# State-space layer: rows normed in three groups, norm weights multiplied on GpSimd and the scale applied on VectorE

## The chip, the cores and the metric

The kernel runs on one core of one Trainium2 chip. The metric is the device time of one execution in microseconds (us). The kernel before has a median of 1499.05 us over three executions (1498.17 to 1500.22). A core has a matmul engine (TensorE, PE in the rows, with its weight loads as PEld), a vector engine (VectorE, DVE), a scalar engine (ScalarE, ACT), a general engine (GpSimd, POOL) and a queue of DMA issues on SyncE (SP). Each engine works through its own queue of instructions in order; an instruction whose input is late holds everything behind it on that engine.

## The reference, cut to what matters

One inference step of a small decoder: one S5 state-space layer, then shared keys and values, then one layer of stick-breaking attention, over 1024 prompt rows and 8 x 8 sample rows of width 1024. Only the start of the state-space layer is touched:

```python
def _rms_norm(x, g):
    y = x32 * lax.rsqrt(jnp.mean(x32 * x32, axis=-1, keepdims=True) + RMS_EPS)
    return (y * g.astype(jnp.float32)).astype(x.dtype)

def _s5_layer(x, ...):
    h = _rms_norm(x, g_pre)
    uz = h @ w_in                      # 1024 x 2048
    u, z = uz[..., :SSM_WIDTH], uz[..., SSM_WIDTH:]
    y, hr, hi = _s5_scan(u, ...)       # needs lam = exp(dt * a), so exp, sin and cos of 64 x 64 parameters
```

## The kernel before, in words

**Tiles of the norm.** The prompt is read as eight tiles t = 0 to 7 of 128 rows x 1024 (`xt`), and the 64 sample rows are a ninth tile, t = 8, which goes first (line 229). For each tile the loop does: one load on SP's queue (line 232); a Square with row sums on ScalarE (line 240); the inverse root of the mean square, `rstd`, called with GpSimd as its engine, so six small operations of one column on GpSimd (lines 77 to 83: a memset, scale and add, a power, and one Newton step of four operations); then one VectorE instruction that multiplies the row scale `rt` and the norm weights `gpre` into the tile (line 243). Eight TensorE transposes of 128 x 128 follow (line 249), in two banks of PSUM (`psb`, three buffers, and `psa`, two). From each bank ScalarE copies a rounded part `xh` (lines 256 and 261) and VectorE subtracts it to get the remainder `xl` (line 205, the helper `tt`). The tile `xt` has five buffers, so that the loads of t = 4 to 7 wait for a tile to be used up.

**What follows.** `xh` and `xl` come in three chunks of columns: chunk 0 has t = 0 to 2, chunk 1 has t = 3 to 5, chunk 2 has t = 6 and 7, each with its part of the samples. A projection `gemm_u(ft)` takes one 128-column block of the weights, split into `whi_u` (ScalarE, line 140) and `wlo_u` (VectorE, line 141), two buffers each, and runs 24 matmuls on each chunk (lines 147 to 149). The third block's `whi_u` needs a buffer that the first block's last matmul frees.

**The parameters.** Beside the norm VectorE computes exp, angles and powers of the layer's parameters (`s5_params`, lines 91 to 1271). ScalarE's Sin (line 1231, after a table load) stands between them. Out of the results come `uu`, and out of `uu` the table `cs` of each round (line 205 in the loop over `ft`), which is copied to `cf` by DMA. `cs` has one buffer, so that the next round's `cs` waits for that copy.

**What sets the order.** The code is traced in the order in which it is written, and a scheduler then places the instructions of each engine by dependencies, its own estimates and the priorities that the code gives (`high_priority`). Queues are in order at run time.

Of the kernel before, what the change touches and what calls it, by code (L numbers as in the profile page):

```python
# [10 lines left out]
F32 = mybir.dt.float32  # L11
# [3 lines left out]
AF = mybir.ActivationFunctionType  # L15
ALU = mybir.AluOpType
# [3 lines left out]
D = 1024  # L20
SEQ = 1024
NS = 8
TS = 8
NTS = NS * TS
L = 8
NC = SEQ // L
W = NC + NS
# [14 lines left out]
ACH = ((0, 3), (3, 3), (6, 2))  # L42
# [27 lines left out]
def rstd(nc, pool, ss, out, n, mul, tag, eng=None):  # L70

    E = eng or nc.vector
    v = pool.tile([128, n], F32, name=f"v_{tag}", tag="rs_v")
    r0 = pool.tile([128, n], F32, name=f"r0_{tag}", tag="rs_r")
    h = pool.tile([128, n], F32, name=f"h_{tag}", tag="rs_h")
    e = pool.tile([128, n], F32, name=f"e_{tag}", tag="rs_e")
    nc.gpsimd.memset(e, -0.5)
    E.tensor_scalar(v, ss, mul, EPS, op0=ALU.mult, op1=ALU.add)
    nc.gpsimd.tensor_tensor(r0, v, e, op=ALU.pow)
    E.tensor_tensor(h, r0, r0, op=ALU.mult)  # L80
    E.tensor_tensor(h, h, v, op=ALU.mult)
    E.tensor_scalar(h, h, -0.5, 1.5, op0=ALU.mult, op1=ALU.add)
    E.tensor_tensor(out, r0, h, op=ALU.mult)
# [117 lines left out]
def s5_layer(tc, nc, io, wp, bank, cst, gains, ident, sgn, zs_d, u_d, y_d, s2):  # L201
    V, Q = nc.vector, nc.gpsimd

    def tt(eng, o, a, b, op):
        eng.tensor_tensor(o, a, b, op=op)

    with ExitStack() as sx:
# [3 lines left out]
        par = st.enter_context(tc.tile_pool(name="a_par", bufs=1, reuse_waits="tile"))  # L211
        s0 = st.enter_context(ExitStack())
        start = s0.enter_context(tc.tile_pool(name="a_start", bufs=1, reuse_waits="tile"))

        def weights(which, ft):

            with tc.high_priority(2 * OFA):
                wraw = wp.tile([128, KT, 128], F32, name=f"wraw_{which}{ft}", tag="wraw", bufs=1)

                (nc.scalar if which == "u" else nc.sync).dma_start(wraw, io["a_win"][ft + (KT if which == "z" else 0)])  # L220
                return split_w(nc, wp, wraw, f"{which}{ft}", [128, KT, 128], Q if which == "z" and ft % 2 else V)


        gpre = start.tile([128, D], F32, name="gpre")
        xh = [big.tile([128, KT, n, W], F32R, name=f"xh{i}") for i, (_, n) in enumerate(ACH)]
        xl = [big.tile([128, KT, n, W], F32R, name=f"xl{i}") for i, (_, n) in enumerate(ACH)]
        xp = io["x_prompt"].rearrange("(c t) d -> t c d", t=L)
        w_first = None
        for t in (8, 0, 1, 2, 3, 4, 5, 6, 7):
            n = 128 if t < 8 else NTS  # L230
            xt = start.tile([128, D], F32, name=f"xt{t}", tag="xt", bufs=5)
            nc.sync.dma_start(xt[:n], xp[t] if t < 8 else io["x_sample"])
            if t == 8:
                nc.sync.dma_start(gpre, io["a_gpre"].to_broadcast([128, D]))
                nc.sync.dma_start(cst, io["consts"][:, 0:129])
            sq = start.tile([128, D], F32, name=f"sq{t}", tag="sq")
            ss = par.tile([128, 1], F32, name=f"ss{t}", tag="ss", bufs=2)
            if n < 128:
                V.memset(ss, 1024.0)
            nc.scalar.activation(sq[:n], xt[:n], AF.Square, accum_out=ss[:n])  # L240
            rt = par.tile([128, 1], F32, name=f"rt{t}", tag="rt", bufs=2)
            rstd(nc, par, ss, rt, 1, 1.0 / D, f"a{t}", Q)
            V.scalar_tensor_tensor(xt[:n], xt[:n], rt[:n], gpre[:n], op0=ALU.mult, op1=ALU.mult)
            for i in range(2):
                ps = bank("a" if i else "b")
                p3 = ps.rearrange("p (a b) -> p a b", a=4)[:, :, :n]
                for j in range(4):
                    k = 4 * i + j
                    nc.tensor.transpose(p3[:, j], xt[:n, k * 128 : (k + 1) * 128], ident[:n, :n])
                ks = slice(4 * i, 4 * i + 4)  # L250
                for c, (t0, m) in enumerate(ACH):
                    if t < 8:
                        if not t0 <= t < t0 + m:
                            continue
                        src, oh, ol = p3, xh[c][:, ks, t - t0, 0:NC], xl[c][:, ks, t - t0, 0:NC]
                        nc.scalar.activation(oh, src, AF.Copy)
                        tt(V, ol, src, oh, ALU.subtract)
                    else:
                        p4 = p3.rearrange("p a (s t) -> p a t s", t=TS)
                        src, oh, ol = p4[:, :, t0 : t0 + m], xh[c][:, ks, :, NC:W], xl[c][:, ks, :, NC:W]  # L260
                        nc.scalar.activation(oh, src, AF.Copy)
                        tt(V, ol, src, oh, ALU.subtract)
            if t == 0:
                w_first = weights("u", 0)

        def gemm(which, ft, evac, w=None):
            wh, wl = w or weights(which, ft)
# [49 lines left out]
        for ft in range(KT):  # L317
            with tc.high_priority(OFA):
# [19 lines left out]
                for i in range(2):  # L338
                    ps = bank("m")
# [11 lines left out]
                ps = bank("m")  # L351
# [1048 lines left out]
```

## Time and profile before

| what | number |
|---|---|
| median of three executions | 1499.05 us |
| the profiled execution's own time | 1500.17 us |
| its span | 1498.4 us |
| busy on PE, DVE, ACT, POOL | 1415.8, 935.0, 718.2, 493.7 us |
| share of the chain that ended last, PE / DVE / POOL / DMA | 75% / 9% / 5% / 4% |

The span is what the trace covers, and 1.8 us of the execution lie outside it. A row of a timeline gives the start, the duration, the engine, the line, the operation, what is written <- what is read, the shape and the count; in brackets stands how long the engine had been idle and what ended that.

### The profile page before, as it was taken

To read this page: it belongs to the slowest core of one execution; us is meant where nothing else is said; L and a number is where in the kernel's file an instruction comes from. 1 tells how busy PE (TensorE), PEld (TensorE's weight loads), DVE (VectorE), ACT (ScalarE), POOL (GpSimd) and SP (SyncE) were. 2 spreads that over 40 slices of the span, in tenths; PEclk is the share of its full clock that TensorE was granted. 3 is DMA by queue.
4 is the path that set the end of the run, shared out by engine and by line. 5 is a ranking of instruction groups with operands and counts; after the bars stand their busy time and mean duration, and the time that the engine had idled before them with its cause. 6 is when DMAs were issued, how large, how long until landed. Compare 5 with 4: busy or idle time off the path is not lost.

```text
span 1498.4 us, 26819 instructions
## 1 busy us (share of the span) xinstructions
PE 1415.8 (94%) x9648; PEld 1145.8 (76%) x9648; DVE 935.0 (62%) x1506; ACT 718.2 (48%) x1424; POOL 493.7 (33%) x473
## 2 busy tenths in 40 slices
PE   4987988899999989999999999999998999998997
PEld 3987978899977889999988877666565665565766
DVE  6877887758755531110122149897888888789545
ACT  5233454454434433332333347676665766576321
POOL 6556565325412132222111012433323233334200
PEclk9999999999999999999999999999999999999999
DMA  5345556674134252232288755979878686754026
GB/s 197 103 129 139 140 126 163 145 251 145 58 106 132 91 224 91 85 123 100 103 314 298 255 201 192 339 284 326 295 257 289 250 308 219 268 190 139 11 82 213
DMA packets 129670, 276.41 MB, mean 184 GB/s; under 512 B 21633, under 2 KB 66562, under 8 KB 129538
## 3 DMA queue, kind: packets, MB, share of 16 engines
q1 hardware_dynamic: 127234, 268.41, 54.0%
q10 hardware_dynamic: 2304, 6.29, 1.3%
q8 instruction: 76, 1.25, 0.3%
q14 instruction: 56, 0.46, 0.1%
HBM read 224.55 MB, written 39.35 MB: 176 GB/s over the span
## 4 chain that ended last, share of the span: by engine, by line
PE 75%; DVE 9%; POOL 5%; DMA 4%; issue 3%; ACT 2%; SPq 1%; DVEq 0%; POOLq 0%; ACTq 0%
PE psmm L147 7%; PE psmm L149 7%; PE psmm L148 7%; PE psqk L147 6%; PE psqk L148 6%; PE psqk L149 6%; PE psa L949 5%; PE psb L1182 5%; PE psb L1164 4%; PE psa L990 4%; PE psqk L1139 3%; PE psqk L1140 2%; DMA cf<-cs 2%; PE psa L147 2%; PE psa L149 2%
## 5 line engine op out<-in xcount | busy, mean ns | idle before, releaser
L1120 POOL TENSOR_TENSOR ql<-q,qh 128x256 fp32r<-128x256 f32 x64 | 62.5, 977 | 285.6 <-ACT qh L1119 246.5
L1141 ACT ACTIVATE F<-psqk,bp 128x384 f32<-128x384 f32 (+2 forms) x192 | 111.3, 580 | 64.6 <-PE psqk L1140 49.2
L1146 DVE TENSOR_TENSOR_SCAN F<-F,maskb 128x256 f32<-128x256 f32 (+3 forms) x128 | 131.2, 1030 | 14.0 <-ACT F L1141 13.6
L1149 POOL TENSOR_TENSOR S<-S,F 128x255 f32<-128x255 f32 (+3 forms) x64 | 100.8, 1574 | 115.7 <-DVE F L1148 22.5
L1142 ACT ACTIVATE S<-psqk,bp 128x384 f32<-128x384 f32 (+2 forms) x192 | 111.4, 583 | 22.7 <-PE psb L1164 22.6
L1164 PE MATMUL psb<-cst,S 128*128 128x128 f32 x576 | 96.7, 285 | 4.4 <-DVE og L1186 3.8
L1164 PEld LDWEIGHTS psb<-cst,S 128*128 128x128 f32 x576 | 67.3, 143 | 35.1 <-issue 20.5
L1148 DVE TENSOR_TENSOR_SCAN F<-F 128x384 f32<-128x384 f32 (+1 forms) x64 | 78.9, 1233 | 20.4 <-ACT F L1141 19.8
L1182 PE MATMUL psb<-at,vr 128*64 128x256 f32 (+1 forms) x640 | 90.0, 369 | 1.2 <-DVE at L1168 1.2
L949 PE MATMUL psa<-vp,sat 128*32 128x256 f32 x1024 | 86.1, 388 | 0.1
L1139 PE MATMUL psqk<-ks,qh 128*128 128x384 f32 (+2 forms) x192 | 77.4, 404 | 6.9 <-DVE ks L1104 5.2
L990 PE MATMUL psa<-kp,qbd 128*32 128x256 f32 x1024 | 75.5, 389 | 0.5 <-PE psb L1164 0.5
L1182 PEld LDWEIGHTS psb<-at,vr 128*64 128x64 f32 x640 | 46.7, 137 | 36.6 <-issue 10.3
L1168 DVE TENSOR_TENSOR at<-psb,maskb 128x384 f32<-128x384 f32 (+3 forms) x128 | 60.3, 478 | 21.3 <-PE psb L1164 20.7
L147 PE MATMUL psmm<-xh,whi_u 128*128 128x408 f32 (+1 forms) x192 | 65.3, 341 | 3.7 <-ACT ut L278 3.1
L147 PE MATMUL psmm<-x,whi_g 128*128 128x408 f32 (+1 forms) x192 | 66.6, 347 | 1.1 <-DVE gt L739 1.1
L943 DVE TENSOR_TENSOR_SCAN sF<-sF 128x513 f32<-128x513 f32 x32 | 44.4, 1388 | 36.1 <-ACT sF L940 35.8
L1139 PEld LDWEIGHTS psqk<-ks,qh 128*128 128x128 f32 x192 | 37.0, 193 | 37.8 <-ACT S L1142 12.8
L1140 PE MATMUL psqk<-ks,ql 128*128 128x384 f32 (+2 forms) x192 | 65.8, 344 | 0.0
L148 PE MATMUL psmm<-xl,whi_u 128*128 128x408 f32 (+1 forms) x192 | 65.4, 341 | 0.0
L149 PE MATMUL psmm<-x,wlo_g 128*128 128x408 f32 (+1 forms) x192 | 64.9, 338 | 0.2 <-DVE wlo_g L141 0.2
L148 PE MATMUL psmm<-x,whi_g 128*128 128x408 f32 (+1 forms) x192 | 65.1, 339 | 0.0
(452 smaller groups left out, 4234.6 us busy)
## 6 DMA issues: line engine op xcount, KB each, us to landing
kp<-cache_kT SPq DMA_DIRECT2D x128, 512.0 KB, 6.0
vp<-cache_v SPq DMA_DIRECT2D x128, 512.0 KB, 5.7
cf<-cs SPq DMA_DIRECT2D x32, 256.0 KB, 5.4
q<-q_d SPq DMA_DIRECT2D x128, 64.0 KB, 4.6
u_d<-ut SPq DMA_DIRECT2D x8, 544.0 KB, 2.8
ug<-u_d SPq DMA_DIRECT2D x64, 68.0 KB, 2.9
y_d<-gt SPq DMA_DIRECT2D x64, 68.0 KB, 2.4
zs_d<-zt SPq DMA_DIRECT2D x8, 544.0 KB, 4.5
```

Of the source, the lines that this page charges most:

```text
L147: nc.tensor.matmul(ps, sh, mh, start=(k == 0), stop=False)
L148: nc.tensor.matmul(ps, sh, ml, start=False, stop=False)
L149: nc.tensor.matmul(ps, sl, mh, start=False, stop=(k == n - 1))
L949: self.nc.tensor.matmul(po[32 * r : 32 * r + 32, 0:256], a[:, 32 * r : 32 * r + 32], rhs[:, r * 256 : (r + 1) * 256], start=start, stop=stop)
L990: nc.tensor.matmul(ps[32 * r : 32 * r + 32, half * 256 : half * 256 + 256], self.qbd[:, 2 * r + e, s, :], kt[:, :, 2 * r + e, :], start=(e ...
L1139: nc.tensor.matmul(ps[:, :m], qh[:, w], ks[:, c0 : c0 + m], start=True, stop=False)
L1141: nc.scalar.activation(F[:, c0 : c0 + m], ps[:, :m], AF.Sigmoid, bias=bp[:, 1, h : h + 1], scale=-0.125)
L1142: nc.scalar.activation(S[:, c0 : c0 + m], ps[:, :m], AF.Sigmoid, bias=bp[:, 0, h : h + 1], scale=0.125)
L1146: V.tensor_tensor_scan(fr, fr, self.maskb[:, 512 - m : 512][:, ::-1], 1.0, ALU.mult, ALU.max)
L1149: (Q if i % 2 else V).tensor_tensor(S[:, 0 : n - 1], S[:, 0 : n - 1], F[:, 1:n], op=ALU.mult)
L1164: nc.tensor.transpose(ps[:, j * 128 : (j + 1) * 128], S[:, (j0 + j) * 128 : (j0 + j + 1) * 128], self.ident)
L1182: nc.tensor.matmul(po[hs, o:256], self.vr[pi][:, j, hs], ats[hh][j // 4][:, j % 4, o:256], start=(j == 0), stop=(j == nj - 1))
```

## The change

Three parts of the norm move. The nine tiles are taken in three groups, (8, 0, 1, 2), (3, 4, 5) and (6, 7). In each group all loads, Squares and a new GpSimd product `xt * gpre` (in place) come first; then one `rstd` for all columns of the group, now on VectorE except for its memset and its power, which stay on GpSimd; then for each tile a VectorE `tensor_scalar` by `rt`, and the transposes as before. `xt` has nine buffers in place of five. `weights("u", 0)` is called behind the first group's `rstd`.

```diff
@@ -70,10 +70,10 @@
 def rstd(nc, pool, ss, out, n, mul, tag, eng=None):
 
     E = eng or nc.vector
-    v = pool.tile([128, n], F32, name=f"v_{tag}", tag="rs_v")
-    r0 = pool.tile([128, n], F32, name=f"r0_{tag}", tag="rs_r")
-    h = pool.tile([128, n], F32, name=f"h_{tag}", tag="rs_h")
-    e = pool.tile([128, n], F32, name=f"e_{tag}", tag="rs_e")
+    v = pool.tile([128, n], F32, name=f"v_{tag}", tag=f"rs_v{n}")
+    r0 = pool.tile([128, n], F32, name=f"r0_{tag}", tag=f"rs_r{n}")
+    h = pool.tile([128, n], F32, name=f"h_{tag}", tag=f"rs_h{n}")
+    e = pool.tile([128, n], F32, name=f"e_{tag}", tag=f"rs_e{n}")
     nc.gpsimd.memset(e, -0.5)
     E.tensor_scalar(v, ss, mul, EPS, op0=ALU.mult, op1=ALU.add)
     nc.gpsimd.tensor_tensor(r0, v, e, op=ALU.pow)
@@ -226,42 +226,49 @@
         xl = [big.tile([128, KT, n, W], F32R, name=f"xl{i}") for i, (_, n) in enumerate(ACH)]
         xp = io["x_prompt"].rearrange("(c t) d -> t c d", t=L)
         w_first = None
-        for t in (8, 0, 1, 2, 3, 4, 5, 6, 7):
-            n = 128 if t < 8 else NTS
-            xt = start.tile([128, D], F32, name=f"xt{t}", tag="xt", bufs=5)
-            nc.sync.dma_start(xt[:n], xp[t] if t < 8 else io["x_sample"])
-            if t == 8:
-                nc.sync.dma_start(gpre, io["a_gpre"].to_broadcast([128, D]))
-                nc.sync.dma_start(cst, io["consts"][:, 0:129])
-            sq = start.tile([128, D], F32, name=f"sq{t}", tag="sq")
-            ss = par.tile([128, 1], F32, name=f"ss{t}", tag="ss", bufs=2)
-            if n < 128:
-                V.memset(ss, 1024.0)
-            nc.scalar.activation(sq[:n], xt[:n], AF.Square, accum_out=ss[:n])
-            rt = par.tile([128, 1], F32, name=f"rt{t}", tag="rt", bufs=2)
-            rstd(nc, par, ss, rt, 1, 1.0 / D, f"a{t}", Q)
-            V.scalar_tensor_tensor(xt[:n], xt[:n], rt[:n], gpre[:n], op0=ALU.mult, op1=ALU.mult)
-            for i in range(2):
-                ps = bank("a" if i else "b")
-                p3 = ps.rearrange("p (a b) -> p a b", a=4)[:, :, :n]
-                for j in range(4):
-                    k = 4 * i + j
-                    nc.tensor.transpose(p3[:, j], xt[:n, k * 128 : (k + 1) * 128], ident[:n, :n])
-                ks = slice(4 * i, 4 * i + 4)
-                for c, (t0, m) in enumerate(ACH):
-                    if t < 8:
-                        if not t0 <= t < t0 + m:
-                            continue
-                        src, oh, ol = p3, xh[c][:, ks, t - t0, 0:NC], xl[c][:, ks, t - t0, 0:NC]
-                        nc.scalar.activation(oh, src, AF.Copy)
-                        tt(V, ol, src, oh, ALU.subtract)
-                    else:
-                        p4 = p3.rearrange("p a (s t) -> p a t s", t=TS)
-                        src, oh, ol = p4[:, :, t0 : t0 + m], xh[c][:, ks, :, NC:W], xl[c][:, ks, :, NC:W]
-                        nc.scalar.activation(oh, src, AF.Copy)
-                        tt(V, ol, src, oh, ALU.subtract)
-            if t == 0:
+        for group in ((8, 0, 1, 2), (3, 4, 5), (6, 7)):
+
+            xts = {}
+            ss = start.tile([128, len(group)], F32, name=f"ss{group[0]}")
+            rt = start.tile([128, len(group)], F32, name=f"rt{group[0]}")
+            V.memset(ss, 1024.0)
+            for e, t in enumerate(group):
+                n = 128 if t < 8 else NTS
+                xt = start.tile([128, D], F32, name=f"xt{t}", tag="xt", bufs=9)
+                xts[t] = xt
+                nc.sync.dma_start(xt[:n], xp[t] if t < 8 else io["x_sample"])
+                if t == 8:
+                    nc.sync.dma_start(gpre, io["a_gpre"].to_broadcast([128, D]))
+                    nc.sync.dma_start(cst, io["consts"][:, 0:129])
+                sq = start.tile([128, D], F32, name=f"sq{t}", tag="sq")
+                nc.scalar.activation(sq[:n], xt[:n], AF.Square, accum_out=ss[:n, e : e + 1])
+                tt(Q, xt[:n], xt[:n], gpre[:n], ALU.mult)
+            rstd(nc, start, ss, rt, len(group), 1.0 / D, f"a{group[0]}")
+            if group[0] == 8:
                 w_first = weights("u", 0)
+            for e, t in enumerate(group):
+                n = 128 if t < 8 else NTS
+                xt = xts[t]
+                V.tensor_scalar(xt[:n], xt[:n], rt[:n, e : e + 1], None, op0=ALU.mult)
+                for i in range(2):
+                    ps = bank("a" if i else "b")
+                    p3 = ps.rearrange("p (a b) -> p a b", a=4)[:, :, :n]
+                    for j in range(4):
+                        k = 4 * i + j
+                        nc.tensor.transpose(p3[:, j], xt[:n, k * 128 : (k + 1) * 128], ident[:n, :n])
+                    ks = slice(4 * i, 4 * i + 4)
+                    for c, (t0, m) in enumerate(ACH):
+                        if t < 8:
+                            if not t0 <= t < t0 + m:
+                                continue
+                            src, oh, ol = p3, xh[c][:, ks, t - t0, 0:NC], xl[c][:, ks, t - t0, 0:NC]
+                            nc.scalar.activation(oh, src, AF.Copy)
+                            tt(V, ol, src, oh, ALU.subtract)
+                        else:
+                            p4 = p3.rearrange("p a (s t) -> p a t s", t=TS)
+                            src, oh, ol = p4[:, :, t0 : t0 + m], xh[c][:, ks, :, NC:W], xl[c][:, ks, :, NC:W]
+                            nc.scalar.activation(oh, src, AF.Copy)
+                            tt(V, ol, src, oh, ALU.subtract)
 
         def gemm(which, ft, evac, w=None):
             wh, wl = w or weights(which, ft)
```

On GpSimd before, `v_a`, `r_a`, `h_a` and `rt` are the steps of `rstd`, one set for each tile (the first two tiles, t = 8 and t = 0, are shown):

```order
L78 TENSOR_SCALAR v_a_104<-ss_100 128x1
L79 TENSOR_TENSOR r_a_105<-v_a_104,e_a_107 128x1
L80 TENSOR_TENSOR h_a_106<-r_a_105 128x1
L77 MEMSET e_a_147 128x1
L81 TENSOR_TENSOR h_a_106<-h_a_106,v_a_104 128x1
L82 TENSOR_SCALAR h_a_106<-h_a_106 128x1
L83 TENSOR_TENSOR rt_103<-r_a_105,h_a_106 128x1
L78 TENSOR_SCALAR v_a_144<-ss_141 128x1
L79 TENSOR_TENSOR r_a_145<-v_a_144,e_a_147 128x1
```

On GpSimd now, with `xt_98` the sample tile, `xt_105` to `xt_115` t = 0 to 2, `xt_208` to `xt_218` t = 3 to 5, and `xt_282`, `xt_287` t = 6 and 7:

```order
L205 TENSOR_TENSOR xt_105<-xt_105,gpre 128x1024
L205 TENSOR_TENSOR xt_110<-xt_110,gpre 128x1024
L205 TENSOR_TENSOR xt_115<-xt_115,gpre 128x1024
L79 TENSOR_TENSOR r_a_121<-v_a_120,e_a_123 128x4
L205 TENSOR_TENSOR xt_208<-xt_208,gpre 128x1024
L205 TENSOR_TENSOR xt_213<-xt_213,gpre 128x1024
L205 TENSOR_TENSOR xt_218<-xt_218,gpre 128x1024
L79 TENSOR_TENSOR r_a_224<-v_a_223,e_a_226 128x3
L205 TENSOR_TENSOR xt_282<-xt_282,gpre 128x1024
L205 TENSOR_TENSOR xt_287<-xt_287,gpre 128x1024
L1297 COPY pk<-h_509 128x64x8
L79 TENSOR_TENSOR r_a_293<-v_a_292,e_a_295 128x2
```

The products of the second and third group stand directly behind the first group's power, which VectorE waits for. On VectorE before, at the start of the norm (`xt_95` is the sample tile, `xt_138` t = 0):

```order
L141 TENSOR_TENSOR wlo_u_173<-wraw_u_170,whi_u_172 128x1024
L243 SCALAR_TENSOR_TENSOR xt_95<-xt_95,rt_103,gpre 64x1024
L205 TENSOR_TENSOR xl_92<-psb_116,xh_89 128x12x8
L205 TENSOR_TENSOR xl_92<-psa_127,xh_89 128x12x8
L205 TENSOR_TENSOR xl_93<-psb_116,xh_90 128x12x8
L243 SCALAR_TENSOR_TENSOR xt_138<-xt_138,rt_143,gpre 128x1024
```

On VectorE now, at the same place:

```order
L141 TENSOR_TENSOR wlo_u_134<-wraw_u_131,whi_u_133 128x1024
L78 TENSOR_SCALAR v_a_120<-ss_95 128x4
L78 TENSOR_SCALAR v_a_223<-ss_205 128x3
L80 TENSOR_TENSOR h_a_122<-r_a_121 128x4
L81 TENSOR_TENSOR h_a_122<-h_a_122,v_a_120 128x4
L82 TENSOR_SCALAR h_a_122<-h_a_122 128x4
L83 TENSOR_TENSOR rt_96<-r_a_121,h_a_122 128x4
L252 TENSOR_SCALAR xt_98<-xt_98,rt_96 64x1024
L252 TENSOR_SCALAR xt_105<-xt_105,rt_96 128x1024
L252 TENSOR_SCALAR xt_110<-xt_110,rt_96 128x1024
L252 TENSOR_SCALAR xt_115<-xt_115,rt_96 128x1024
L1219 TENSOR_SCALAR aim<-pr,cst 128x64
```

Four tiles are now scaled one behind the other, after four dependent small operations; the first `xl` comes behind them and behind four more instructions.

## Rows read from the trace of the kernel before

**Rows 1.** Chain that ended last, 0 to 75 us: start, duration, what

```profile
23.03 1.54 POOL r_a L79
...
36.83 1.28 DVE xt L243
...
49.71 0.14 PE psmm L148
...
49.87 1.07 ACT whi_u L140
...
50.97 1.23 DVE wlo_u L141
...
52.59 1.28 ACT L1231
...
57.92 3.31 POOL cma_g L126
```

**Rows 2.** Windows: length, busy PE, PEld, DVE, ACT, POOL (count), clock, DMA, GB/s

```profile
80.00:320.00 240.00, 209.97 (x1428) 200.58 (x1427) 180.22 (x302) 107.36 (x239) 130.71 (x101) 0.96 0.58 141
320.00:1498.00 1178.00, 1148.85 (x7901) 891.16 (x7899) 694.45 (x1047) 578.42 (x1124) 317.36 (x273) 0.99 0.56 196
```

**Rows 3.** Timeline of ScalarE, the Square of t = 0

```profile
11.10 1.06 ACT L240 ACTIVATE sq<-xt 128x1024 f32<-128x1024 f32 x1 [2.77 <-DMA xt<-x_prompt]
```

**Rows 4.** The tile of norm weights: its load and landing

```profile
L234 SPq DMA_DIRECT2D gpre<-a_gpre x1: 564/564/564, 1.4 to 1.4; - x1
...
DMA to landing us min/median/max: 6.1/6.1/6.1
```

**Rows 5.** Timeline of GpSimd: a power, a copy, a product of 128 x 1024

```profile
12.61 0.56 POOL L79 TENSOR_TENSOR r_a<-v_a,e_a 128x1 f32<-128x1 f32 x1
...
19.45 0.65 POOL L1290 COPY pk<-h 128x512 f32<-128x512 f32 x1
...
220.46 2.35 POOL L141 TENSOR_TENSOR wlo_z<-wraw_z,whi_z 128x1024 fp32r<-128x1024 f32 x1 [0.55 <-ACT whi_z L140]
```

**Rows 6.** Timeline of VectorE, scales by a column, and t = 2's norm

```profile
16.10 0.24 DVE L1212 TENSOR_SCALAR aim<-pr,cst 128x64 f32<-128x64 f32 x1
...
19.55 1.62 DVE L243 SCALAR_TENSOR_TENSOR xt<-xt,rt,gpre 128x1024 f32<-128x1024 f32 x1
...
120.36 0.33 DVE L328 TENSOR_SCALAR sb<-sb,cst 128x256 f32<-128x256 f32 x1
```

**Rows 7.** Groups by line, VectorE, 0 to 400 us: busy us, mean ns

```profile
L205 DVE TENSOR_TENSOR l<-psb,ts 128x3 f32<-128x3 f32 x16 | 2.4, 150 | 0.0
```

**Rows 8.** Timeline of VectorE and GpSimd side by side, 203 to 212 us

```profile
205.04 1.06 POOL L205 TENSOR_TENSOR m<-uu 128x512 f32<-128x512 f32 x1
205.61 2.17 DVE L205 TENSOR_TENSOR wb<-sb,wri 128x256 f32<-128x256 f32 x2
206.17 1.32 POOL L205 TENSOR_TENSOR cs<-cs,m 128x512 f32<-128x512 f32 x1
...
209.23 1.68 DVE L205 TENSOR_TENSOR ep<-pk,wb 128x1024 f32<-128x1024 f32 x1
209.80 1.71 POOL L205 TENSOR_TENSOR tb<-tb,cf 128x256 f32<-128x256 f32 x1
```

**Rows 9.** Timeline of both engines, three instructions with the other engine out of the way

```profile
66.59 0.30 POOL L131 TENSOR_TENSOR cmc_g<-uu,sc 128x64 f32<-128x64 f32 x1
...
104.87 1.22 DVE L205 TENSOR_TENSOR tm<-pk,wb 128x1024 f32<-128x1024 f32 x1
...
129.70 0.41 DVE L205 TENSOR_TENSOR wb<-sb,wri 128x256 f32<-128x256 f32 x1
```

**Rows 10.** Timeline of VectorE, remainders of t = 6 and 7

```profile
41.81 0.68 DVE L205 TENSOR_TENSOR xl<-psb,xh 128x512 fp32r<-128x512 f32 x1
42.41 0.68 DVE L205 TENSOR_TENSOR xl<-psa,xh 128x512 fp32r<-128x512 f32 x1
```

**Rows 11.** Who waited for whom, 60 to 320 us: total us, times, longest

```profile
PE psa L435 <- ACT gt L437: 10.0, 4, 5.0
```

## The prediction, on record before the changed kernel ran

> **What bounds the kernel now.** I read the windows first. From 320 us on TensorE is busy for 1148.85 of 1178 us, so nothing that happens in the norm can be won or lost there; from 80 to 320 us it is busy for 209.97 of 240, so the state-space rounds have some 30 us in which they wait for something else [rows 2]. Then the chain that ended last, in its first 75 us. The reader is to see three stretches in it. Up to 36.8 us it runs through GpSimd's small operations of the norm, and these are not always cheap: a power takes 1.54 us [rows 1] where another takes 0.56 [rows 5]. Then, from t = 7's norm on VectorE at 36.83, it goes through the remainders and the first block's matmuls, which end at 49.85. At 49.87 ScalarE makes the third block's `whi_u` in the buffer that these matmuls free, VectorE makes `wlo_u` (1.23 us), and ScalarE's table load for Sin begins at 52.59. Behind Sin stand `uu`, `cs` and all rounds [rows 1]. So the change reaches the end only through two moments: when the first block of u is done on TensorE (49.85) and when the table load begins (52.59). I work out where both land.
>
> **What the change removes and adds.** GpSimd loses six small operations for each tile and gets nine products of 128 x 1024. VectorE loses nine instructions that multiply scale and weights at once (1.28 us for the last of them [rows 1], 1.62 for t = 2 [rows 6]) and gets nine scales by a column, three sets of five small operations, and memsets that lie in its idle start. No such product on GpSimd is in the trace of before, but the nearest has the same shape: 2.35 us [rows 5]. A VectorE scale of 128 x 1024 isn't there either. From below: 0.24 us at 64 columns and 0.33 at 256 [rows 6] give 0.47 ns a column, so 0.33 + 768 x 0.47 ns = 0.69 us. From above: 1.28 us, the instruction that it replaces. I take 0.69, since both of its rows are the same operation. A small operation on four columns costs what one on three does, 0.15 us [rows 7]; a power 0.56, and the copy of `h` that now stands in the queue 0.65 [rows 5].
>
> **First group, up to its power.** The norm weights land at 1.4 + 6.1 = 7.5 us [rows 4], and the sample tile's product, 2.35 us, is done by 9.9. The product overwrites its tile, so that t = 0's waits until the Square has read it: 11.10 + 1.06 = 12.2 [rows 3]. Then GpSimd is the bound: t = 0 ends at 14.5, t = 1 at 16.9, `v_a` slips in (0.15), t = 2 ends at 19.4, the power at 20.0. In the kernel before t = 2 was scaled by 19.55 + 1.62 = 21.2 [rows 6]. Up to here there is no loss. The nine loads now stand ahead of the parameters' loads on SP's queue, and none waits for a buffer any more; I cost that at nothing, since VectorE comes to the first of the parameters (`aim`) only behind the four scales. Without that cover it would be up to some 2 us.
>
> **What stands behind that power.** GpSimd goes straight on with the products of t = 3 to 5, the second power, the products of t = 6 and 7 and the copy. VectorE has four small operations that depend on each other, then four scales. Do the two engines run side by side? The trace shows that they don't when both take SBUF tensors: two `wb` that take 0.41 us each alone [rows 9] took 2.17 together. The first waited for GpSimd's `m` to end at 206.10, ran to about 206.4, and the second waited for `cs`, which had got in between and ended at 207.49. `ep` at 209.23 took 1.68 us in place of the 1.22 of a like product (`tm`) alone, and then `tb` on GpSimd was held until `ep` had ended [rows 8, 9]. That is strict turns, one instruction each, though VectorE had the next one ready. So the sum by turns: from 20.0, five products 11.75, a power 0.56, the copy 0.65, four small operations 0.6, four scales 2.76: the first group is scaled at 36.3 us, 15.1 later than before. In this stretch eight instructions of VectorE stand against eight of GpSimd with the first power, so that each finds one ahead of it. Who waits for VectorE there: the transposes of the first group on TensorE, behind them `xh` on ScalarE, and all of the parameters, which are on VectorE itself.
>
> The Trainium skill says the same of the ports: its page "SBUF — State Buffer", section "Who interferes with whom", has it that the pair of ports which VectorE and GpSimd share is a lock held for a whole instruction, taken by a VectorE instruction with two SBUF inputs or in a two-port mode, and that whoever comes second blocks fully. By that rule the sum is the 36.3 above. One row speaks against it as a rule of turns: `cma_g`, 128 x 64, took 3.31 us [rows 1] where its like takes 0.30 alone [rows 9], so GpSimd was kept out through a whole run of short VectorE instructions; by that row VectorE would wait once and then go through.
>
> **From there to the two moments.** Up to the last remainder VectorE has these in its queue: 16 remainders at a pitch of 0.60 [rows 10], 9.6 us; five scales, 3.45; three long ones of about 1.2 (`wlo_u` of the second block, `dd`, its reduction), 3.6; and 57 short ones (the samples' remainders, the exp and angle steps, the two other groups' `rstd`) at 0.15 [rows 7] or a little over, 9.2. That is 26 us without a gap, so the last remainder stands at 62.3. Twelve matmuls of the last chunk are left, at 0.14 each by the row at 49.71 [rows 1], 1.7 us: the first block ends at 64.0 in place of 49.85, 14.1 later. ScalarE's queue now has Sin's table load directly behind the third `whi_u`, so it begins at 64.0 + 1.07 = 65.1 in place of 52.59, 12.5 later; `wlo_u` has gone behind the exp steps and is late for no one but the projection.
>
> Both ends of the unknown: if VectorE waits for GpSimd once and then goes through, the group is scaled at 20.0 + 2.35 + 0.6 + 2.76 = 25.7, and four products, 9.4 us, are left to run beside the rest. The remainders read one tensor from PSUM, and I take them as not held; the other instructions are, so about half of the 9.4 I count as waits: 30.4 in effect, and a table load 6.6 later than before. If nothing waits for anything, the group is scaled at 23.4 and the table load is 0.4 earlier than before. I take 11 us, near the end of strict turns, since rows 8 show turns where GpSimd has a queue of long instructions, which is the case here, and the other row has short ones on both sides.
>
> **Behind the table load.** Everything up to 320 us hangs on Sin's results or on TensorE, and both are late by about the same; I let the delay through whole. Against the profiled execution's own time that is 1500.17 + 11 = 1511.2; the median of the runs lies 1.1 below that execution, so I forecast 1510.
>
> **Rivals.** 1. *Side by side.* GpSimd's products cost VectorE nothing. For it: VectorE's remainders read one tensor from PSUM, and in these it may not meet GpSimd at all. Against: the pairs that met for a turn each [rows 8]. Price: a table load 0.4 earlier, and 2 more if VectorE's 26 us are 24: 1496.7 to 1498.7, no measurable change. 2. *The rounds take it up.* TensorE has 30 idle us between 80 and 320, and if these are waits that a later start does not lengthen, the end moves by 0 to 3: about 1500. Against: the rounds' own chain starts at Sin, and it is late too. 3. *Faster: the new order of the rounds.* The scheduler has reordered them as well; TensorE's state matmuls (`psa`) stood for 10.0 us behind ScalarE's `gt` [rows 11], and if these come at a better place in its queue, all of that goes. With the cheaper end of the norm, 6.6, it is 1499.05 + 6.6 - 10.0 = 1495.7. It decides once more is won there than is lost in front; nothing in the trace of before says that it happens, and the reorder can as well go the other way (1516).
>
> **How the numbers follow.** Turns between the engines 0.70 (1505 to 1514 on its own), a worse order on top of that 0.05 (1516), side by side 0.10, taken up 0.07, faster by the order 0.08. A measurement of this kernel can tell about 0.2% (3 us) from no change, so slower is 0.75, same 0.17, faster 0.08. The range goes from 1498, which leaves out the case of 1495.7 and some of the side by side, to 1516.
>
> **What would show it.** Right: VectorE's four operations behind the first power (lines 80 to 83) start more than 1.5 us apart, each with a product of GpSimd ending before it; the first transposes of t = 2 at about 36 us; the third `whi_u` at about 63 and the table load at about 65; from 320 us on no difference in TensorE's time. Wrong: these four within 1 us, and the table load near 52. Wrong in the second half: a table load 11 us late with an end that is not.

## The result and the profile after

The changed kernel takes 1514.58 us (median of four, 1513.25 to 1515.35), the kernel before 1499.12 us on the same chip (four, 1498.17 to 1500.22): a ratio of 1.0102, 95% interval 1.0084 to 1.0119, so 1.0% slower. 1510 us was forecast, with a range of 1498 to 1516. The profiled execution took 1513.25 us with a span of 1511.5, 13.1 us more than the span before; the medians stand 15.5 apart.

GpSimd's queue in the changed kernel, as a timeline (start, duration, engine, line, operation, what is written <- read, shape, count; in brackets idle time before it):

```profile
12.74 6.96 POOL L205 TENSOR_TENSOR xt<-xt,gpre 128x1024 f32<-128x1024 f32 x3 [2.72 <-ACT sq L244]
19.66 1.03 POOL L79 TENSOR_TENSOR r_a<-v_a,e_a 128x4 f32<-128x4 f32 x1
20.64 6.95 POOL L205 TENSOR_TENSOR xt<-xt,gpre 128x1024 f32<-128x1024 f32 x3
27.53 1.11 POOL L79 TENSOR_TENSOR r_a<-v_a,e_a 128x3 f32<-128x3 f32 x1
28.36 5.22 POOL L205 TENSOR_TENSOR xt<-xt,gpre 128x1024 f32<-128x1024 f32 x2
33.53 1.08 POOL L1297 COPY pk<-h 128x512 f32<-128x512 f32 x1
```

And VectorE's beside it:

```profile
20.72 2.29 DVE L80 TENSOR_TENSOR h_a<-r_a 128x4 f32<-128x4 f32 x1 [0.99 <-POOL r_a L79]
23.05 2.27 DVE L81 TENSOR_TENSOR h_a<-h_a,v_a 128x4 f32<-128x4 f32 x1
25.34 2.27 DVE L82 TENSOR_SCALAR h_a<-h_a 128x4 f32<-128x4 f32 x1
27.65 0.16 DVE L83 TENSOR_TENSOR rt<-r_a,h_a 128x4 f32<-128x4 f32 x1
27.85 7.31 DVE L252 TENSOR_SCALAR xt<-xt,rt 64x1024 f32<-64x1024 f32 x4
```

A product takes 6.96 / 3 = 2.32 us. Each of three operations on four columns, worth 0.16 us, takes 2.3: its product's length. The four scales take 7.31 us, between them two products and the copy. Rows 8 showed turns between instructions of 0.4 to 1.3 us [rows 8]; here the same turns are held by long ones. The three products beside the small operations took 6.95 us, no longer than the three ahead of the power (6.96), so the small operations cost GpSimd nothing. The first group is scaled at 35.16 us; in the kernel before t = 2 was scaled at 21.2 [rows 6].

What TensorE then does, its first transposes:

```profile
28.65 0.69 PE L258 MATMUL psb<-cst,xt 64*128 64x64 f32 x4 [28.65 <-DVE xt L252]
...
31.42 1.11 PE L258 MATMUL psb<-cst,xt 128*128 128x128 f32 x4 [1.66 <-DVE xt L252]
...
34.18 1.12 PE L258 MATMUL psb<-cst,xt 128*128 128x128 f32 x4 [0.80 <-DVE xt L252]
39.14 1.12 PE L258 MATMUL psb<-cst,xt 128*128 128x128 f32 x4 [3.84 <-DVE xl L205]
```

The 2.77 us from one tile to the next are a little less than a scale and a product one behind the other (0.69 + 2.32 = 3.01), so the two turns overlap by some 0.2 us. The fourth row is the fourth use of `psb`, which has three buffers: t = 2 was scaled at 35.16, but its transposes waited until 39.14 for a remainder `xl` that frees the bank. ScalarE, where the two moments of the prediction stand (to be read against 49.87 and 52.59 in [rows 1]), and its last eviction of a z block (the copy of the last result of z out of PSUM):

```profile
62.97 1.06 ACT L140 ACTIVATE whi_u<-wraw_u 128x1024 fp32r<-128x1024 f32 x1 [2.25 <-PE psmm L148]
64.04 1.28 ACT L1238 ACT_TABLE_LOAD   x1
...
65.34 0.69 ACT L1238 ACTIVATE sc<-an 128x576 f32<-128x576 f32 x1
...
344.07 0.38 ACT L288 ACTIVATE zt<-psmm 128x272 f32<-128x272 f32 x1
```

The same eviction in the kernel before:

```profile
329.94 0.38 ACT L281 ACTIVATE zt<-psmm 128x272 f32<-128x272 f32 x1
```

The windows of the changed kernel (length, busy PE, PEld, DVE, ACT, POOL with counts, clock, DMA share, GB/s):

```profile
0.00:80.00 80.00, 43.30 (x245) 41.23 (x246) 60.72 (x162) 31.14 (x55) 39.67 (x42) 1.00 0.34 118
80.00:320.00 240.00, 209.08 (x1416) 200.39 (x1415) 182.54 (x312) 104.97 (x239) 141.28 (x111) 0.96 0.57 141
320.00:345.00 25.00, 25.00 (x154) 24.99 (x153) 12.32 (x10) 14.18 (x18) 5.08 (x3) 1.00 0.95 340
335.00:1511.00 1176.00, 1147.44 (x7900) 890.61 (x7898) 682.75 (x1046) 575.77 (x1122) 313.76 (x272) 0.99 0.56 194
```

and the first and third of them in the kernel before:

```profile
0.00:80.00 80.00, 57.03 (x323) 54.07 (x324) 60.34 (x159) 32.45 (x61) 45.64 (x99) 0.94 0.47 147
320.00:345.00 25.00, 24.50 (x148) 24.26 (x147) 12.97 (x10) 14.81 (x17) 5.08 (x2) 1.00 0.90 347
```

TensorE does 13.7 us less in the first 80 us (57.03 - 43.30). Counted in matmuls it is 78 fewer (323 - 245); the busy time also holds the granted clock, whose mean in that window was 0.94 before and is 1.00 now. From 80 to 320 us it does the same as before (209.08 against 209.97 [rows 2]), though it still has 31 idle us there, and at the end it is as full as before [rows 2]. So the 13.7 us of front are not made up: the last z eviction is 14.1 us late, the span 13.1.

### The profile page after: what moved, and what is told of

Its sections match the earlier page's. It is cut to its first block, busy times and chain, and to the rows that moved or that the text cites. A ratio compares the mean times of both kernels' runs of the same rounds, so it can differ in the third digit from the quotient of the medians.

```text
span 1511.5 us, 26767 instructions
## 1 busy us (share of the span) xinstructions
PE 1414.8 (94%) x9648; PEld 1147.2 (76%) x9648; DVE 930.3 (62%) x1523; ACT 718.2 (48%) x1424; POOL 499.3 (33%) x425
## 4 chain that ended last, share of the span: by engine, by line
PE 74%; DVE 11%; DMA 6%; POOL 3%; issue 3%; ACT 2%; SPq 1%; ACTq 0%; DVEq 0%; POOLq 0%
PE psmm L147 7%; PE psmm L148 7%; PE psmm L149 7%; PE psqk L147 6%; PE psqk L148 6%; PE psqk L149 6%; PE psa L956 5%; PE psb L1189 5%; PE psa L997 4%; PE psb L1171 4%; PE psqk L1146 3%; PE psqk L1147 2%; PE psa L147 2%; PE psa L149 2%; PE psa L148 2%
## 5 line engine op out<-in xcount | busy, mean ns | idle before, releaser
L1153 DVE TENSOR_TENSOR_SCAN F<-F,maskb 128x256 f32<-128x256 f32 (+3 forms) x128 | 132.1, 1037 | 14.2 <-ACT F L1148 13.7
L1175 DVE TENSOR_TENSOR at<-psb,maskb 128x384 f32<-128x384 f32 (+3 forms) x128 | 60.2, 478 | 21.2 <-PE psb L1171 20.6
L147 PE MATMUL psmm<-x,whi_g 128*128 128x408 f32 (+1 forms) x192 | 66.6, 347 | 1.1 <-DVE gt L746 1.1
L147 PE MATMUL psmm<-xh,whi_z 128*128 128x408 f32 (+1 forms) x192 | 65.4, 341 | 0.2 <-ACT zt L288 0.2
L149 PE MATMUL psmm<-xh,wlo_z 128*128 128x408 f32 (+1 forms) x192 | 65.2, 340 | 0.0
```

What stands on the lines that cost most here:

```text
L147: nc.tensor.matmul(ps, sh, mh, start=(k == 0), stop=False)
L149: nc.tensor.matmul(ps, sl, mh, start=False, stop=(k == n - 1))
L1153: V.tensor_tensor_scan(fr, fr, self.maskb[:, 512 - m : 512][:, ::-1], 1.0, ALU.mult, ALU.max)
```

## The experiments

Two questions were open. Is it the products beside VectorE's queue, or the grouping itself (a tile waits for three others)? And which of the two late moments carries the end: TensorE's front, or Sin with the parameters' chain behind it? The table has one row for each kernel: its ratio to the kernel before over all its executions, and from its one profile TensorE's work in the first 80 us, the start of Sin, the start of the last z eviction, and the span (all in us). The executions of one kernel spread over 2 to 7 us, so two spans that differ by less say little by themselves.

| kernel | ratio, 95% interval | TensorE, 0 to 80 | Sin | last z | span |
|---|---|---|---|---|---|
| before | 1 | 57.03 | 53.88 | 329.94 | 1498.4 |
| changed | 1.0102, 1.0084 to 1.0119 | 43.30 | 65.34 | 344.07 | 1511.5 |
| 1, no products | 0.9997, 0.9988 to 1.0005 | 53.90 | 56.28 | 332.16 | 1499.6 |
| 2, products alone | 1.0166, 1.0149 to 1.0183 | 26.49 | 47.13 | 355.38 | 1523.3 |
| 3, rstd on GpSimd | 1.0182, 1.0167 to 1.0198 | 23.38 | 44.79 | 358.56 | 1525.4 |
| 4, double products | 1.0252, 1.0238 to 1.0266 | 15.78 | 67.94 | 368.44 | 1537.3 |
| 5, five products later | 1.0091, 1.0075 to 1.0106 | 44.56 | 61.92 | 343.96 | 1512.7 |
| 6, products of first group | 1.0033, 1.0022 to 1.0043 | 49.79 | 58.02 | 335.29 | 1502.2 |
| 7, products of later groups | 1.0092, 1.0078 to 1.0106 | 46.63 | 63.16 | 343.15 | 1511.6 |
| 8, tile by tile | 1.0006, 0.9997 to 1.0015 | 56.93 | 51.36 | 331.74 | 1498.1 |
| 9, before, parameters later | 1.0036, 1.0022 to 1.0049 | 57.20 | 57.60 | 330.90 | 1502.2 |
| 10, as 8, parameters later | 1.0064, 1.0046 to 1.0082 | 58.08 | 58.71 | 334.08 | 1505.5 |
| 11, Sin behind first block | 1.0017, 1.0008 to 1.0025 | 59.03 | 63.80 | 322.52 | 1501.1 |
| 12, first group in two | 0.9969, 0.9958 to 0.9980 | 54.68 | 53.76 | 327.60 | 1495.4 |

### 1. No products on GpSimd

```diff
-                tt(Q, xt[:n], xt[:n], gpre[:n], ALU.mult)
-                V.tensor_scalar(xt[:n], xt[:n], rt[:n, e : e + 1], None, op0=ALU.mult)
+                V.scalar_tensor_tensor(xt[:n], xt[:n], rt[:n, e : e + 1], gpre[:n], op0=ALU.mult, op1=ALU.mult)
```

> The three groups stay, but GpSimd gets no products: VectorE multiplies scale and weights at once, as before the change. Turn-taking: with nothing long in GpSimd's queue the four small operations behind the first power start about 0.15 us apart (2.3 us in the changed kernel), the first group is scaled at about 21 to 24 us in place of 35.2, Sin's table load begins before 56 us, and the time is 1496 to 1502 us. Grouping itself (the wait for four tiles): the products do not matter, the time stays at 1509 to 1515. A worse order of the rounds: the rounds are ordered nearly as in the changed kernel, so the front is early but the end stays above 1507.

VectorE in this run:

```profile
16.31 0.16 DVE L80 TENSOR_TENSOR h_a<-r_a 128x4 f32<-128x4 f32 x1 [1.21 <-POOL r_a L79]
16.50 0.16 DVE L81 TENSOR_TENSOR h_a<-h_a,v_a 128x4 f32<-128x4 f32 x1
...
17.10 4.87 DVE L251 SCALAR_TENSOR_TENSOR xt<-xt,rt,gpre 64x1024 f32<-64x1024 f32 x4
```

The same operations take 0.16 us, the first group is scaled at 21.97, and all of the loss is gone (ratio 0.9997). The table load (54.99) came as expected. The groups of four, three and two stand, so grouping costs nothing that can be measured against the kernel before, and the products are the cause.

### 2. The products alone, without groups

```diff
 # kernel before
+            tt(Q, xt[:n], xt[:n], gpre[:n], ALU.mult)
-            V.scalar_tensor_tensor(xt[:n], xt[:n], rt[:n], gpre[:n], op0=ALU.mult, op1=ALU.mult)
+            V.tensor_scalar(xt[:n], xt[:n], rt[:n], None, op0=ALU.mult)
```

> The kernel before (a rstd on GpSimd for each tile, no groups) with one part of the change alone: GpSimd multiplies each tile by the norm weights, VectorE scales it by its column. Turn-taking: GpSimd's queue is 9 x 2.35 = 21 us longer and in series with each tile's rstd, VectorE's scales wait for products; t = 7 is scaled at 45 to 57 us in place of 38.1, and the time is 1506 to 1520 us. Grouping itself: without groups the time is that of before, 1497 to 1502.

It was slower than expected, 1525.12 us: the products stand in one queue with each tile's `rstd`, and the last scale, of t = 7, is at

```profile
74.06 2.64 DVE L244 TENSOR_SCALAR xt<-xt,rt 128x1024 f32<-128x1024 f32 x1
```

against 45 to 57 expected. The change's move of `rstd` off GpSimd made the products cheaper: run 3, which has the groups but not that move, is as slow as this one. Sin came 6.8 us earlier than before and the end 25 us later.

### 3. The groups' rstd on GpSimd

```diff
-            rstd(nc, start, ss, rt, len(group), 1.0 / D, f"a{group[0]}")
+            rstd(nc, start, ss, rt, len(group), 1.0 / D, f"a{group[0]}", Q)
```

> The changed kernel with all of the three groups' rstd on GpSimd in place of VectorE. The small operations then stand in GpSimd's queue behind the products of later groups, while VectorE has nothing to wait for and does the parameters' exp and angle steps first: Sin's table load comes early (before 40 us) and the first block of u late (70 to 85 us, against 62.9). If TensorE's idle front sets the end, the time is 1518 to 1535 us, and the last z matmul is late by as much as the end. If the parameters' chain behind Sin sets it, the time is 1492 to 1502 us.

Here the two moments go apart. The table load, Sin, and TensorE's first instruction (three rows of the timeline):

```profile
31.01 1.28 ACT L1238 ACT_TABLE_LOAD   x1 [8.25 <-DVE wlo_u L141]
...
44.79 0.68 ACT L1238 ACTIVATE sc<-an 128x576 f32<-128x576 f32 x1 [12.49 <-DVE an L1236]
...
48.53 0.69 PE L258 MATMUL psb<-cst,xt 64*128 64x64 f32 x4 [48.53 <-DVE xt L252]
```

The table load comes before 40 us, as expected; Sin then waits 12.49 us for its angles and is 9.1 us earlier than before. The first block of u was done at 87 us, 2 us past its range, and the end is 27.0 us later, within the range for TensorE's front. A late front is enough to make the end late, however early the parameters are. TensorE did 33.7 us less by 80 us, so 0.8 of each lost us arrives at the end (in run 2, 24.9 of 30.5, as much).

### 4. Each product twice

```diff
+        ones = start.tile([128, D], F32, name="ones")
+        V.memset(ones, 1.0)
                 tt(Q, xt[:n], xt[:n], gpre[:n], ALU.mult)
+                tt(Q, xt[:n], xt[:n], ones[:n], ALU.mult)
```

> The changed kernel with each product on GpSimd followed by a second one, by a tile of ones (nine instructions of 128 x 1024 more on GpSimd, one memset on VectorE, same values). Turn-taking: 9 x 2.35 = 21 us more of GpSimd's long instructions ahead of or beside VectorE's queue; less what is hidden, the end comes 12 to 25 us later than the changed kernel's, 1526 to 1540 us, and TensorE's idle time in the first 80 us grows by as much as the end moves. If GpSimd's products matter only by the first group's wait, under 1520.

1538.0 us, 23.4 above the changed kernel's median, as expected by turns. TensorE's work by 80 us falls by another 27.5. Each held operation of VectorE still waits for one product. The first two steps behind the power start two products apart (4.68 us), since the third group's `v_a` now stands between them in VectorE's queue and waits for a product too:

```profile
22.18 2.29 DVE L80 TENSOR_TENSOR h_a<-r_a 128x4 f32<-128x4 f32 x1 [0.41 <-POOL r_a L79]
...
24.53 2.30 DVE L78 TENSOR_SCALAR v_a<-ss 128x2 f32<-128x2 f32 x1
...
26.86 2.29 DVE L81 TENSOR_TENSOR h_a<-h_a,v_a 128x4 f32<-128x4 f32 x1
```

### 5. The products of the second and third group later

```diff
-                tt(Q, xt[:n], xt[:n], gpre[:n], ALU.mult)
+                tt(Q, xt[:n], xt[:n], gcur[0][:n], ALU.mult)   # gpre for the first group, then gp2
+                V.tensor_scalar(hold, rt[:, 3:4], 0.0, 1.0, op0=ALU.mult, op1=ALU.add)
+                    V.tensor_scalar(gp2, gpre, hold, None, op0=ALU.mult)   # behind t = 2's scale
```

> The changed kernel, but the products of the second and third group read a copy of the norm weights that VectorE makes from them behind the first group's rstd, so that none of these five products can stand beside the first group's rstd. Same instructions otherwise (two VectorE instructions more). Turn-taking: the four small operations behind the first power start about 0.15 us apart, the first group is scaled at 24 to 27 us in place of 35.2, and the time is 1501 to 1509 us, a part of the loss being left since the five products come later, beside the remainders. Grouping itself: 1511 to 1516, as the changed kernel or worse.

The small operations took 0.16 us and the first group was scaled at 25.6, as expected; the time did not follow (1514.0 us). VectorE behind the first group:

```profile
22.93 2.72 DVE L257 TENSOR_SCALAR xt<-xt,rt 64x1024 f32<-64x1024 f32 x4
...
26.48 2.38 DVE L91 TENSOR_SCALAR ex_dt<-pr 128x96 f32<-128x96 f32 x1
...
30.46 3.18 DVE L205 TENSOR_TENSOR dd<-dd,cst 16x1024 f32<-16x1024 f32 x1
...
34.17 1.71 DVE L82 TENSOR_SCALAR h_a<-h_a 128x3 f32<-128x3 f32 x1
...
35.93 2.34 DVE L93 TENSOR_SCALAR ex_dt<-ex_dt 128x96 f32<-128x96 f32 x1
```

and TensorE, which stops twice for a remainder that stands behind these in VectorE's queue:

```profile
34.30 1.11 PE L266 MATMUL psb<-cst,xt 128*128 128x128 f32 x4 [6.71 <-DVE xl L205]
38.93 1.11 PE L266 MATMUL psa<-cst,xt 128*128 128x128 f32 x4 [3.52 <-DVE xl L205]
```

The five products only found other victims: four instructions that take 0.19, 1.21, 0.15 and 0.19 us in the changed kernel, where they come behind the products, took 9.6 together here. The expectation failed in taking a later product for a cheaper one. The remainders, which read one tensor from PSUM, are not held themselves (0.67 us at 33.57 and at 38.20, in the middle of the products), but VectorE's queue is in order.

### 6 and 7. Products of the first group alone, and of the others alone

```diff
+                if group[0] == 8:   # run 6; run 7: !=
                     tt(Q, xt[:n], xt[:n], gpre[:n], ALU.mult)
+                if group[0] == 8:   # run 6; run 7: !=
                     V.tensor_scalar(xt[:n], xt[:n], rt[:n, e : e + 1], None, op0=ALU.mult)
+                else:
+                    V.scalar_tensor_tensor(xt[:n], xt[:n], rt[:n, e : e + 1], gpre[:n], op0=ALU.mult, op1=ALU.mult)
```

> The changed kernel with products on GpSimd for the first group only (samples, t = 0 to 2); the other two groups are scaled and weighted at once by VectorE. Turn-taking: these four products run while VectorE has nothing to do and set only the time of the first power (about 20 us, against 15.3 without products), so that the small operations behind it start about 0.15 us apart, and a part of the 4.5 us is hidden: 1501 to 1505 us. If products cost by their number wherever they stand, four of nine cost 6 us: 1506.

> The reverse: no products for the first group, GpSimd's products for t = 3 to 7 only, queued directly behind the first power. Turn-taking: the power is early (about 16 us), but the four small operations behind it are about 2.3 us apart again, five products (11.8 us) stand beside VectorE's queue: first group scaled at 28 to 33 us, time 1509 to 1513. By number, five of nine: 1508. If only the lateness of the first power mattered: 1500.

Run 6 took 1504.96 us, at the edge of its range: four products ahead of the power cost 4.6 us, no more than the power's delay (its small operations begin at 21.30, in run 1 at 16.31). Run 7 took 1513.39, at the edge of its range too. Its power is as early as in run 1, but

```profile
16.34 2.29 DVE L80 TENSOR_TENSOR h_a<-r_a 128x4 f32<-128x4 f32 x1 [1.21 <-POOL r_a L79]
18.67 2.26 DVE L81 TENSOR_TENSOR h_a<-h_a,v_a 128x4 f32<-128x4 f32 x1
...
23.46 4.87 DVE L256 SCALAR_TENSOR_TENSOR xt<-xt,rt,gpre 64x1024 f32<-64x1024 f32 x4
28.25 2.33 DVE L78 TENSOR_SCALAR v_a<-ss 128x3 f32<-128x3 f32 x1
```

Behind three products the four long instructions ran free, 4.87 us as in run 1, while GpSimd's fourth product waited for its Square until 27.31: contention and its absence in one run. The five products beside VectorE's queue alone bring nearly the whole loss (1.0092 of 1.0102). The two parts do not add up to the changed kernel's loss (4.6 and 13.0 against 15.5). Run 7 scales its first group 7 us before the changed kernel does and still ends where that ends; why its last 3 us of TensorE's front bring nothing stays open.

### 8. Groups of one tile, no products

```diff
-        for group in ((8, 0, 1, 2), (3, 4, 5), (6, 7)):
+        for group in ((8,), (0,), (1,), (2,), (3,), (4,), (5,), (6,), (7,)):
 # and the edit of run 1
```

> Groups of one tile, no products on GpSimd, small operations on VectorE (the power on GpSimd), scale and weights at once on VectorE. Against the run without products in groups of 4, 3 and 2 this takes the grouping away alone. If the grouping costs (tiles wait for others), TensorE's first instruction comes at about 11 us in place of 18, and TensorE does more in the first 50 us: 1493 to 1498 us. If the 36 small operations more on VectorE (0.15 us each, 5 us) and the round trips to the power weigh as much, 1498 to 1503.

1500.42 us: TensorE begins at 12.48 in place of 18.43 and does 3.0 us more by 80 us, and the end is the same as run 1's. The first block of u was done 6.5 us later than in the kernel before (the third `whi_u` began at 56.42), without a cost; TensorE had done as much by 80 us as there (56.93 against 57.03). So the end does not hang on that block alone. Nor does it follow TensorE's work by 80 us for one: run 1's 3.0 us less cost nothing either.

### 9 to 11. The parameters later, the norm untouched

```diff
     nc.sync.dma_start(pr, io["s5_par"])
+    V.tensor_scalar(pr, pr, hold, None, op0=ALU.mult)
 # hold: rt * 0 + 1 of t = 7 (run 9 on the kernel before, run 10 on run 8's);
 # run 11, on the kernel before: from the first block of u
```

> The kernel before with one edit: the state-space parameters are multiplied by a one that comes from t = 7's rstd, so that VectorE's exp and angle steps stand behind the norm's work (two VectorE instructions more, same values). It takes some 30 short instructions (about 5 us) out of VectorE's queue ahead of the last remainders, and makes Sin late. If TensorE's idle time in front is all that sets the end: TensorE does 2 to 6 us more in the first 50 us, and the time is 1494 to 1498 us though Sin comes as late as before or later. If the parameters' chain behind Sin sets it: 1500 to 1506.

> The same edit in the run with groups of one tile and no products on GpSimd, where Sin came 2.5 us earlier than before and the first block of u 6.5 us later, at the same end. TensorE's front: the first block's end moves from 56.4 back to about 50, TensorE does 2 to 6 us more in the first 80 us, 1494 to 1499 us. The parameters' chain: 1501 to 1508.

> The kernel before with the state-space parameters multiplied by a one that is made from the first block of u (two VectorE instructions more, same values): all exp and angle steps stand behind that block's end, and nothing of the norm is touched. TensorE's front is as before or a little earlier (57 to 59 us of work in the first 80 us), and Sin comes at 60 to 66 us, 6 to 12 us late (in the changed kernel 11.5). If the parameters' chain behind Sin delays the end by itself, one for one: 1506 to 1513 us. If TensorE's front alone sets it: 1497 to 1502.

Runs 9 and 10 did not give TensorE the 2 to 6 us more in front that were expected (0.2 more than before, 1.2 more than run 8). They were slower, though TensorE's front was no later: 1505.03 us, within the range for the parameters' chain, and 1509.28, 1.3 above it. Against their bases Sin came 3.7 and 7.4 us later and the span grew by 3.8 and 7.4 (the medians by 4.7 and 8.9): here the end moved with the parameters' chain, about one for one. Run 11 then moved Sin by 9.9 us, nearly as far as the change did:

```profile
63.80 0.69 ACT L1236 ACTIVATE sc<-an 128x576 f32<-128x576 f32 x1
...
322.52 0.38 ACT L283 ACTIVATE zt<-psmm 128x272 f32<-128x272 f32 x1
```

with this window behind it:

```profile
320.00:345.00 25.00, 19.07 (x93) 16.87 (x92) 12.74 (x9) 13.39 (x15) 5.01 (x2) 0.86 0.93 321
```

The z matmuls were done 7.4 us earlier than before, and then TensorE stood idle for 5.9 of 25 us, in the kernel before 0.5: with the filling work used up, what is left of the rounds is late. The time is 1502.72 us, 0.17% above and between the two ranges expected, the span 2.7 us longer for 9.9 us of Sin, with TensorE 2 us ahead in front. So either moment can move the end: the last z eviction where TensorE's front is late, the rounds behind Sin where it is not. Sin's price lies between 0.3 and 1 us for one; the scheduler places the rounds anew in each of these kernels, and what in that spread is their order and what is Sin the runs do not tell apart.

### 12. The first group in two

```diff
-        for group in ((8, 0, 1, 2), (3, 4, 5), (6, 7)):
+        for group in ((8, 0), (1, 2), (3, 4, 5), (6, 7)):
 # and the edit of run 1
```

> The run without products on GpSimd, with the first group split in two (samples and t = 0; t = 1 and 2): VectorE multiplies scale and weights at once, small operations once per group on VectorE. TensorE's first instruction comes at 12 to 15 us in place of 18.4, with 20 small VectorE operations fewer than tile by tile. Both moments, TensorE's front and Sin, come as early as in any run so far: 1496 to 1500 us, at best 0.2% faster than before; if waits elsewhere take it up, 1500.

1495.92 us, at the lower edge of its range, 0.3% faster than the kernel before (0.9958 to 0.9980) and the best of all. Its front is not the best (54.68 us by 80 us, first instruction at 15.34). TensorE makes it up between 80 and 320 us, where it does 216.66 us against 209.97 [rows 2]. Among its waits, 60 to 320 us, is the one that rival 3 named, to be read against 10.0 us in [rows 11]:

```profile
PE psa L441 <- ACT gt L443: 3.6, 4, 1.6
```

In run 1, with the same instructions but for the first group's split, it was

```profile
PE psa L441 <- ACT gt L443: 10.2, 4, 3.8
```

That the order of the rounds gave these 3 us and not something else was not tried by itself.

## Why the prediction was right, step by step

**The first group up to its power** was forecast to end at 20.0 us and ended at 20.7.

**The turns** were forecast as one instruction each, and the first group as scaled at 36.3; it was at 35.16. Three of the four small operations waited for a product; the fourth didn't, while GpSimd stood at its second power. The sum added the small operations to the products, beside which they ran. The sign for t = 2's first transposes, about 36 us, did not come: they began at 39.14, behind a remainder. Runs 1, 5 and 6 show the cause: without a product in GpSimd's queue the same operations take 0.16 us. The rule of the Trainium skill's page "SBUF — State Buffer", section "Who interferes with whom", a lock held for the whole instruction, fits to within the 0.2 us by which two turns overlap: an operation of 0.16 us took 2.27 to 2.29.

**The size was off.** The sum by turns gave 14.1 us at the first block and 12.5 at the table load; I took 11 for both and for the end, and forecast 1510. Measured were 13.1 at the first block (62.97 against 49.87), 11.45 at the table load and 13.1 at the end of the profiled executions. So the sum by turns was about 1.0 too long at both moments, and the 11 was close at the table load. That is luck: it had been moved towards the cheaper end because of `cma_g` [rows 1], and in the timeline the turns came one for one. The mis-sized term is this 11 as the delay of the end, 2.1 too small. Most of the rest of the 4.6 us from 1510 to 1514.58 lies in the executions: I took the median 1.1 below the profiled execution, and here it was 1.3 above.

**From there to the two moments.** VectorE's stretch without a gap, forecast as 26 us to 62.3, took 24.8 and ended at 59.9; scales of 128 x 1024 took 0.69 us as estimated (2.07 for three). Behind it the forecast had 12 matmuls, 1.7 us; there were nearly twice as many, and the third `whi_u` began 3.0 us later. The two errors partly cancel: the first block's end was forecast at 64.0.

**Which moment carries the end** was left open in the prediction ("both are late by about the same"), and there the path was only half told. By runs 2 and 3 a late TensorE front makes the end late with an early Sin, at 0.8 us for one: 11 of the 13.1 us for the change's 13.7. (That rate is not fixed: it was 0.5 in run 6, 0.9 in run 4 and 1.3 in run 7, where Sin was late too.) By runs 9 to 11 a late Sin does so with an early front, at 0.3 to 1 for one: 3 to 11 us for the change's 11.5. So each could have brought most of the loss by itself, and they do not add up. For the front speaks that TensorE's added idle time lies there (13.7 us by 80 us, 0.9 from 80 to 320) and that it is full beside its last z work (25.00 of 25 us, in run 11 19.07). Against it speaks the profile's own chain, which in the changed kernel runs through Sin's table load, as before (and as in run 11, where 9.9 us of Sin cost 2.7):

```profile
64.04 1.28 ACT L1238
...
68.76 9.02 POOL cma_g L126
```

So that the front carried the end in the changed kernel is argued, not shown, and how much Sin adds there no run shows. Neither the first block's end nor TensorE's work by 80 us is the measure by itself: the block was 6.5 us late in run 8 and the work 3.1 us less in run 1, both at no cost.

**The rivals.** Side by side: ruled out by the timeline and run 1. The rounds take it up: in part, for the parameters' chain. The first of the `cf` copies, which hang on Sin, is issued 11.6 us late (93.6 against 82.0) and the last 7.3 late (283.9 against 276.6); but as much time as TensorE lost in front was lost at the end. Faster by the order of the rounds: not in the changed kernel, where TensorE's wait for `gt` fell from 10.0 to 7.4 us only; in run 12 the wait went to 3.6 and the end came 3.0 us earlier.

## What to carry to other kernels

Long GpSimd instructions on SBUF are not free beside a VectorE queue of short dependent ones: each such instruction can cost a product's whole length (2.3 us for one of 0.16), and in run 5 moving the products later only changed which instruction paid. Placed where VectorE had nothing to do, they still cost 4.6 us by delaying the power (run 6). Left on VectorE, the work took 1.22 us in place of 0.69 for a tile and the end was not later (run 1). And do not count on idle time of the matmul engine later on to take up work that is lost in front: here 13.7 us were lost by 80 us and 13.1 at the end, though run 1 lost 3.1 and nothing at the end.

## What was not expected of the hardware

Who gets the next turn is not settled by "one each". In the changed kernel's scales VectorE and GpSimd took turns one for one; but from 68.76 us GpSimd's `cma_g` of 128 x 64, alone 0.30 us [rows 9], took 9.02 us

```profile
68.76 9.02 POOL L126 TENSOR_TENSOR cma_g<-uu,sc 128x64 f32<-128x64 f32 x1 [1.60 <-DVE uu L133]
```

while VectorE was busy without a gap with 34 instructions, all but the last of them under 0.5 us:

```profile
68.76:77.74 8.98, 8.85 (x34) 1.00 0.19 76
```

In runs 1 and 12 it took 8.04 and 8.56 us, in the kernel before and run 11 3.31 and 3.30 and `cmb_g` behind it 5.4. So a run of ready short instructions on VectorE can keep GpSimd out, while the dependent small operations let it in after each. What divides the two cases stays open: the four scales do not depend on one another either, and GpSimd got in between them. No run tested it.
